# A fused attention block on one core: later weight scans, sooner gate casts, another order at the second step of a batch

## Chip, core and metric

The kernel runs on one core of one Trainium2 chip. The metric is device time in microseconds, from the start to the end of one execution. The engines named below are TensorE (PE, matmuls), VectorE (DVE), ScalarE (ACT), GpSimd (POOL) and SyncE (SP, which issues DMAs).

## What is computed

One encoder layer over 1024 tokens of width 1024. A projection `h = x @ W_in` gives queries, keys, values and gates for two groups of eight heads with 64 columns each. Group a attends within a two-dimensional neighbourhood (rows of 64 tokens, a window of 8 x 16) with a learned bias; group b attends within 128 positions, with rotary positions, a learned sink, and keys and values shared by four heads.

```python
s = einsum(q_r, k_win) * scale + bias              # group a, per grid row
s = where(|i - j| <= 128, einsum(q, k_band) * scale, MASK); s = concat(s, sink)   # group b
y = einsum(softmax(s), v)
mixed = concat([y_a * silu(z_a), y_b * silu(z_b)])
x = layer_norm(alpha * x + mixed @ W_out) * gain + bias
```

Matmul operands are float16 pairs, a high and a low part. Each product is three matmuls: high x high, high x low and low x high. So every operand is scaled, cast (the high half, mostly on ScalarE) and subtracted (the low half, on VectorE or GpSimd), and the scales need the largest absolute value of the weights: that is a scan.

## The kernel before, in words

A first part of about 120 us loads x and the weights, computes the values and projects the first six tiles of 128 columns. Then comes the main loop, which the change is about; a final part finishes the output projection, the residual and the normalisation.

The loop runs over 128 units: 64 of group b, then 64 of group a. A unit is 128 queries of one head with all the keys that they see. Four units make a batch, so there are 32 batches (also called quads, number q covers steps 4q to 4q+3). The loop is written as steps `i`, one per unit, and the engines' orders follow the order in which a step's code emits instructions:

- `batch` and `stage_mm` (L930) emit the score products of four units into PSUM banks with tag `s`, of which there are five. This is done at the end of the step before the batch.
- `stage_qk` (L955, VectorE) adds the bias or mask and takes the row's extreme, into `sn` and `nm`.
- `stage_exp` (L971, ScalarE) takes the exponentials and their sums, for most units back into the PSUM bank; the third unit of a batch goes to an SBUF tile `px`.
- `stage_sum` (L977 and L978, VectorE) makes the reciprocals `ri` of two units' sums.
- `stage_tr` scales and splits the probabilities: high half on ScalarE (L989), low half on VectorE (L990), then a transposing DMA on SyncE (L996) into `tr`.
- `stage_pv` (L1032) multiplies by the values, into one half of the single bank `t`; batch q's comes at step 4q+11 (`PV_AT`), right after the next scores.
- `stage_z` (L1040 and L1043, VectorE) multiplies that half by the gates, at step 4q+13 (`Z_AT`).

Between these, `pump_to` feeds TensorE with other matmuls, spread over the steps by the table `FILL_AT`: first the remaining projections (`FILL`, 48 matmuls of 512 columns each, L401, two PSUM banks with tag `pj`), then the first parts of the output projection (`out_head`, L1162). Evacuations of projected tiles, weight splits (`w_split`, L211 to L217), scans and casts wait in queues, one for each engine; `pop` takes a few of them per step, those with the smaller `prio` first.

Of the output weights, `wo_load` brings in the raw tiles at steps `WO_LD`, `wo_scan` (L430) takes the absolute sums, `wo_max` at step `WO_MAX` combines them, a transpose in the batch that starts at `WO_MAX + 4` and `wo_scale` make the scale, and `wo_split` (`WO_AT`, L1118 to L1131) casts. `m_queue` (`M_AT`, L1146 and L1147) casts the finished gate products of group b, two ScalarE casts and two GpSimd subtractions for each of four tiles. `big_tile` hands out slots of the tags `xb` and `xc`, four each, which held weights before.

Of the kernel before, what the change touches and what calls it, by code (L numbers as in the profile page):

```python
# [38 lines left out]
SCALE_AT = ((4, 6), (7, 2))  # L39
K_ORDER = (5, 0, 6, 1, 7, 2, 3, 4)  # L40
FILL = ORDER[NPRO:]
FILL_AT = [0, 8, 17, 25, 33, 41, 49, 57, 65.5, 74, 82, 90, 98, 106, 113, 121, 124, 126, 128, 131, 136]
ZTAG = {"z3": "zv", "zb3": "zc", "z2": "zs", "zb1": "zd", "zb2": "ze"}
X2POOL = (1, 3, 5)
WVPOOL = (3, 5)
# [1 line left out]
WIN_AT = [186, 202, 218, 234]  # L47
VA_AT = [46, 49, 52, 55]
WO_TAG = ("wor", "wor", "raw", "raw") + ("wr",) * 5 + ("wor", "wor", "raw", "raw", "raw", "wr", "wr")
M_AT = [105, 112, 118, 120]  # L50
WO_PRE = (9, 10, 12, 13, 14, 15)
WO_POST = (7, 8)
WO_MAX = 72
EO = (4, 5, 6, 7, 0, 1, 2, 3)
LAST = ((0, 384), (384, 128))
NPE = 384
PRE_AT = (12, 20)
WARP = (0, 0.33, 0.54, 0.86, 1)
QK_AT = 0.75
WO_AT = [80, 84, 88, 92, 128, 129, 130, 131]  # L60
WO_LD = [18, 22, 26, 30, 36, 39, 42, 45, 48, 112, 116, 33, 130, 130]
WIN0 = (0, 8, 24, 40)
WINW = (24, 32, 32, 24)
# [8 lines left out]
def hybrid_block(ctx, tc, xT, x, wt, wv, wo, bias, sink, gain, lbias, cos, sin, bmask, out):  # L72
# [4 lines left out]
    big = ctx.enter_context(tc.tile_pool(name="big", bufs=4))  # L77
# [15 lines left out]
    def big_tile(name, shape, dt):  # L93
        n = taken[0]
        taken[0] += 1
        return big.tile(list(shape), dt, tag="xb" if n % 8 < 4 else "xc", name=name)

    xh, xl, x1, x1pair, x16h, x16l = {}, {}, {}, [], {}, {}
    for k in range(KT):
# [65 lines left out]
    def enq(eng, fn, *deps, prio=1, after=0):  # L165
        op = Op(eng, fn, deps, prio)
        if clock["step"] is not None:
            queues[eng].append(op)
        elif after:
            events.setdefault(ran[0] + after, []).append(op.emit)  # L170
        else:
            op.emit()
        return op
# [3 lines left out]
    def pop(eng, n, top=1, late=0):  # L177
        q = queues[eng]
        ready = [op for op in q if op.prio <= top and all(
            d.step is not None and d.step + d.lag < clock["step"] + late for d in op.deps)]  # L180
        ready = sorted(ready, key=lambda op: op.prio)[:n]
        for op in ready:
            q.remove(op)
            op.emit()
        return len(ready)
# [243 lines left out]
    def wo_scan(n):  # L429
        nc.scalar.activation(scrap[:, :512], wo_raw[n], AF.Abs, accum_out=wom[:, n:n + 1])  # L430
# [501 lines left out]
    def stage_qk(u):  # L932
        g, p, j, t = u
        n, _c = geom(u)
        ps = st[u, "ps"]
        m, end = n, 384
        if g == "a":
            b, half = t
            m, end = NROW[half] * WINW[b], 384 if half else 384 - WINW[1]
            bias_t, op = st.pop((u, "b"))  # L940
            need(op)
            init = 3e38
        else:
            bias_t = bm[:, 128 if t == 0 else 0:(128 if t == 0 else 0) + n]
            h = 2 * p + j
            init = nsk[:, h:h + 1]
        s0 = sns[units.index(u) % 2]
        sn = s0[:, end - m:]
        if g == "b" and t == 0:
            nc.vector.tensor_copy(s0[:, 384:385], nsk[:, h:h + 1])  # L950
        elif units.index(u) == 64:
            nc.vector.memset(s0[:, 384 - WINW[1]:384], -NEG)
        nm = ap.tile([128, 1], F32, tag="nm", name="nm", bufs=6)
        c = min(p, 1) if g == "b" else 2
        nc.vector.tensor_tensor_reduce(sn[:, :m], ps[:, :m], bias_t, sg[:, c:c + 1], init,  # L955
                                       op0=ALU.add, op1=ALU.min, accum_out=nm)
        st[u, "sn"] = sn
        st[u, "nm"] = nm

    def stage_exp(u):  # L960
        n, _c = geom(u)
        m = n + 1 if u[0] == "b" else n
        sn, nm = st.pop((u, "sn")), st.pop((u, "nm"))
        pt = st[u, "bank"] = st.pop((u, "ps"))
        if units.index(u) % 4 == 2:
            pt = ap.tile([128, 388], F32, tag="px", name="px", bufs=1)
        k = units.index(u) % 2
        if units.index(u) % 2 == 0:
            st["sm"] = ap.tile([128, 2], F32, tag="sm", name="sm", bufs=4)
        sm = st["sm"][:, k:k + 1]  # L970
        nc.scalar.activation(pt[:, :m], sn[:, :m], AF.Exp, bias=nm, scale=-1.0, accum_out=sm)  # L971
        st[u, "p"] = pt

    def stage_sum(us):
        ri, sm = ap.tile([128, 2], F32, tag="ri", name="ri", bufs=4), st["sm"]
        c = st.pop((us[1], "bank"))[:, 508:510]
        nc.vector.tensor_scalar_mul(c, sm, 1.0 / PSCALE)  # L977
        nc.vector.reciprocal(ri, c)  # L978
        for k, u in enumerate(us):
            st[u, "ri"] = ri[:, k:k + 1]  # L980
# [166 lines left out]
            m_ops[e].append(enq("pool", lambda h=h: nc.gpsimd.tensor_sub(  # L1147
                ml[e][:, h], zt[e][:, h], mh[e][:, h]), o))

    LO = 8  # L1150
    NU = len(units)
    def out_mms(t, a, ps, es, c=None):
        o, w = (0, 512) if c is None else LAST[c]
# [162 lines left out]
        stage_mm(us)  # L1316

    PV_AT = {4 * q + 11: q for q in range(30)}
    PV_AT.update({131: 30, 133: 31})
    Z_AT = {4 * q + 13: q for q in range(30) if q not in (24, 25)}  # L1320
    Z_AT.update({115: 24, 116: 25, 132: 30, 134: 31})

    clock["step"] = 0
    scan_ops = []
    for i in range(-LD, NU + LO):
        if 0 <= i + LD < NU:
            stage_load(units[i + LD], i)
        if i < 0:
            continue
        clock["step"] = i  # L1330
        per, h = divmod(i, 16)
        bulk["step"] = i
        if i in VA_AT:
            gather_v(0, VA_AT.index(i))
        for n in range(len(WO_LD)):
            if WO_LD[n] == i:
                load_ops["wo", n] = enq("sp", lambda n=n: wo_load(n), wo_ops.get({9: 0, 10: 1, 12: 2, 13: 3}.get(n)),
                                        w_ops.get(17 + n if 4 <= n <= 8 else None))
                if n not in WO_PRE + WO_POST:
                    scan_ops.append(enq("act", lambda n=n: wo_scan(n), load_ops["wo", n]))  # L1340
        if i in PRE_AT:
            n = len(WO_PRE) - len(PRE_AT) + PRE_AT.index(i)
            scan_ops.append(enq("act", lambda n=n: wo_pre(n)))
        if i == WO_MAX - 6:
            for n in WO_POST:
                scan_ops.append(enq("act", lambda n=n: wo_scan(n), load_ops["wo", n]))
        if i == WO_MAX:
            need(*scan_ops)
            wo_max()
        for n in range(len(WO_AT)):  # L1350
            if WO_AT[n] == i:
                wo_split(n)
        if i == 131:
            enq("sp", gain_load, *m_ops[4])
        if i in M_AT:
            m_queue(4 + M_AT.index(i))
        if bulk["last"] != i or (queues["sp"] and i - queues["sp"][0].born > 2):
            pop("sp", 1 if i < 118 else 3)
        if i < NU:
            if i == 0:  # L1360
                batch(0)
                stage_qk(units[0])
            if i % 4 != 3:
                stage_qk(units[i + 1])
        if i in Z_AT and i % 4 == 3:
            stage_z(Z_AT.pop(i))
        if i > Z3_END:
            pop("dve", 1, 0)
        if i % 4 and i < NU:
            stage_exp(units[i])  # L1370
        early = pop("act", 1, 0) if i % 4 == 1 else 0
        if i % 4 == 1 and i < NU:
            stage_sum(units[i - 1:i + 1])
        if i in Z_AT:
            stage_z(Z_AT.pop(i))
        if i % 4 == 1 and i < NU:
            for u in units[i - 1:i + 1]:
                stage_tr(u)
        if i % 4 == 0 and 4 <= i <= NU:
            for u in units[i - 2:i]:  # L1380
                stage_tr(u)
        early = early or pop("act", 1, 0)
        if i in M_SCALE:
            m_scale(M_SCALE.index(i))
        if WO_MAX + 4 <= i < WO_MAX + 7:
            wo_scale(i - WO_MAX - 4)
        pump_to(i + F1)
        if i - 1 in PV_AT and quad(PV_AT[i - 1])[0] == "a":
            _, p, b = quad(PV_AT[i - 1])
            if p < 3:  # L1390
                gather_v(p + 1, b)
        free = 2 if i % 4 > 1 or i >= NU else 0
        turned = pop("dve", free if i < M_AT[1] else 1 + free)
        if i % 4 == 0 and i < NU:
            stage_exp(units[i])
        if i in PV_AT or i % 4 == 3 and i + 1 < NU:
            if i < NU:
                stage_sum(units[i - 1:i + 1])
            pump_to(i + QK_AT)
            if i + 1 < NU:  # L1400
                batch(i + 1)
            if i in PV_AT:
                stage_pv(PV_AT[i])
            if i + 1 < NU:
                stage_qk(units[i + 1])
        pop("act", max(free + (1 if free and (i >= M_AT[0] or len(queues["act"]) > 4) else 0) - early, 0))
        if not turned:
            pop("dve", 1, 0, 1)
        pop("pool", NP)
        pump_to(i + 1)  # L1410
# [78 lines left out]
```

## Time and profile before

| | us |
|---|---|
| median of 3 runs | 447.92 (447.80 to 448.05) |
| the profiled execution | 448.15 |
| its span, first to last instruction | 446.3 |
| TensorE busy | 434.3 |
| VectorE busy | 347.3 |
| ScalarE busy | 298.5 |
| GpSimd busy | 212.3 |

The profile is one execution. A row of the timeline gives start, duration, engine, line of the kernel, operation, what it writes and reads, the shape and a count of merged instructions; in brackets stands how long the engine had been idle and what ended that. A row of the groups ends in busy time, mean ns of one, and idle time before. A row of the windows gives the stretch, its length, and busy time with the count of instructions for PE, PEld, DVE, ACT and POOL, then the granted clock, the DMA share and GB/s. The granted TensorE clock was 0.999 of full speed.

### The profile page before, as it was taken

The numbers are of one execution on the slowest core, as the hardware profiler recorded it, in microseconds if no ns is written. First come the engines' busy times: TensorE is split into PE (matmuls) and PEld (weight loads), VectorE is DVE, ScalarE is ACT, GpSimd is POOL, SyncE is SP. The second block draws the span as 40 slices with busy tenths as digits, with TensorE's granted clock in tenths as the row PEclk, the third lists the DMA queues.
The fourth block names the chain that finished last, engine by engine and source line by source line (L and its number), as shares of the span: only waits on it lengthen the run. The fifth ranks groups of instructions, "written<-read, shape, count | busy, mean of one in ns | idle before, by whom it ended". The sixth has DMA issues, their size and how long they took to land. (4 is left out here: it accounts for less than half of the span.)

```text
span 446.3 us, 8786 instructions
## 1 busy us (share of the span) xinstructions
PE 434.3 (97%) x2955; PEld 233.7 (52%) x2955; DVE 347.3 (78%) x897; ACT 298.5 (67%) x697; POOL 212.3 (48%) x204
## 2 busy tenths in 40 slices
PE   9999999999998999999999999999999989999994
PEld 9987754444444444444544555454545544444442
DVE  5999948649978888898888888877758849089953
ACT  7798269766588888888867978787867794002211
POOL 1206734546835737557505436654555358005740
PEclk9999999999999999999999999999999999999999
DMA  8991078977946867796978999998898989001711
GB/s 298 325 359 51 25 263 252 320 252 241 317 95 136 140 146 176 128 139 151 172 152 191 166 176 226 200 217 174 213 238 170 193 151 393 6 0 72 258 73 70
DMA packets 133981, 81.72 MB, mean 183 GB/s; under 512 B 101296, under 2 KB 113328, under 8 KB 133680
## 3 DMA queue, kind: packets, MB, share of 16 engines
q1 hardware_dynamic: 133504, 80.67, 72.3%
q8 instruction: 23, 0.38, 0.4%
q10 hardware_dynamic: 432, 0.49, 0.3%
q14 instruction: 22, 0.18, 0.2%
HBM read 50.73 MB, written 9.96 MB: 136 GB/s over the span
## 5 line engine op out<-in xcount | busy, mean ns | idle before, releaser
L401 PE MATMUL ps_pj<-xf,wh 128*128 128x512 f16 x672 | 200.5, 379 | 0.0
L401 PE MATMUL ps_pj<-xf,wl 128*128 128x512 f16 x336 | 127.6, 380 | 0.0
L401 PEld LDWEIGHTS <-wh 128*128 128x128 f16 x672 | 65.2, 98 | 75.0 <-issue 0.5
L989 ACT ACTIVATE split<-ps_s,ri 128x384 f16<-128x384 f32 (+2 forms) x96 | 48.4, 538 | 22.5 <-issue 9.7
L990 DVE SCALAR_TENSOR_TENSOR split<-ps_s,ri,split 128x384 f16<-128x384 f32 (+2 forms) x96 | 52.0, 569 | 12.8 <-ACT split L989 12.8
L1162 PEld LDWEIGHTS <-m 128*128 128x128 f16 x408 | 38.7, 98 | 43.7
L971 ACT ACTIVATE ps_s<-sn,nm 128x385 f32<-128x385 f32 (+3 forms) x96 | 52.1, 543 | 12.7 <-DVE nm L955 11.4
L1162 PE MATMUL ps_s<-wo,m 128*128 128x512 f16 (+1 forms) x240 | 53.3, 374 | 0.0
L401 PEld LDWEIGHTS <-wl 128*128 128x128 f16 x336 | 32.8, 98 | 38.9 <-issue 0.6
L216 POOL TENSOR_SCALAR wr<-wr,wsc 128x512 f32<-128x512 f32 x26 | 22.3, 859 | 50.9 <-ACT wh L211 50.6
L930 PE MATMUL ps_s<-ks,qs 64*128 64x384 f16 (+4 forms) x384 | 36.9, 305 | 3.2 <-DVE split L990 2.9
L955 DVE CUSTOM_DVE_ANT_0 sn<-ps_s,bm,nsk 128x384 f32<-128x384 f32 (+1 forms) x64 | 39.6, 633 | 0.1
L955 DVE CUSTOM_DVE_ANT_0 sn<-ps_s,bias,sg 128x264 f32<-128x264 f32 (+1 forms) x64 | 33.9, 546 | 6.9 <-PE ps_s L930 6.4
L898 POOL TENSOR_SCALAR bias<-bias,rsg 128x552 f32<-128x552 f32 (+1 forms) x24 | 19.8, 826 | 40.1 <-DMA bias<-in_bias 31.4
L217 POOL TENSOR_TENSOR wl<-wr,wh 128x512 f16<-128x512 f32 x26 | 31.9, 1228 | 2.2
L1219 ACT ACTIVATE sd<-mv,eps 128x1 f32<-128x1 f32 x8 | 2.4, 294 | 44.5 <-DVE mv L1217 42.2
L930 PEld LDWEIGHTS <-qs 64*128 64x128 f16 x384 | 16.8, 94 | 25.6 <-issue 19.2
L1261 POOL TENSOR_TENSOR xr<-xr,gb 128x512 f32<-128x512 f32 x7 | 11.2, 1608 | 36.0 <-ACT xr L1258 36.0
L990 DVE SCALAR_TENSOR_TENSOR split<-px,ri,split 128x384 f16<-128x384 f32 (+2 forms) x32 | 27.2, 849 | 1.3 <-ACT split L989 1.3
L678 PEld LDWEIGHTS <-xf 128*128 128x128 f16 x216 | 21.0, 98 | 8.4 <-DVE xf L532 0.3
L977 DVE TENSOR_SCALAR ps_s<-sm 128x2 f32<-128x2 f32 x64 | 10.2, 160 | 18.7 <-ACT ps_s L971 18.3
L1162 PE MATMUL ps_pj<-wo,m 128*128 128x512 f16 (+1 forms) x120 | 24.2, 347 | 0.0
(213 smaller groups left out, 803.1 us busy)
## 6 DMA issues: line engine op xcount, KB each, us to landing
ws<-in_wt SPq DMA_DIRECT2D x15, 512.0 KB, 5.5
wr<-in_wt SPq DMA_DIRECT2D x26, 256.0 KB, 3.2
bias<-in_bias SPq DMA_DIRECT2D x16, 276.0 KB, 3.3
wor<-in_wo SPq DMA_DIRECT2D x16, 256.0 KB, 3.4
xr<-in_x SPq DMA_DIRECT2D x8, 512.0 KB, 7.5
xraw<-in_xT SPq DMA_DIRECT2D x15, 256.0 KB, 4.9
out<-xr SPq DMA_DIRECT2D x14, 256.0 KB, 2.0
bias<-in_bias SPq DMA_DIRECT2D x8, 368.0 KB, 3.6
```

The lines of the kernel that those rows point to most:

```text
L216: nc.gpsimd.tensor_scalar(raw, raw, scale, 1.0, op0=ALU.mult, op1=ALU.mult)
L217: nc.gpsimd.tensor_sub(l, raw, h)
L401: nc.tensor.matmul(ps, a[:, k % 4, :], mv, start=(k == 0 and i == 0), stop=(k == KT - 1 and i == 2))
L678: nc.tensor.matmul(ps[:, :320], lh[t // 4, k][:, 128 * (t % 4):128 * (t % 4) + 128], rh[k][:, 320 * a:320 * a + 320], start=(k == first an ...
L898: op = enq("pool", lambda: nc.gpsimd.tensor_scalar(bv, bv, rsg, -1.0, op0=ALU.mult, op1=ALU.mult), ld, prio=0)
L930: nc.tensor.matmul(st[u, "ps"][:, :m], *parts[i], start=i == 0, stop=i == 2)
L955: nc.vector.tensor_tensor_reduce(sn[:, :m], ps[:, :m], bias_t, sg[:, c:c + 1], init, op0=ALU.add, op1=ALU.min, accum_out=nm)
L971: nc.scalar.activation(pt[:, :m], sn[:, :m], AF.Exp, bias=nm, scale=-1.0, accum_out=sm)
L989: nc.scalar.activation(hl[:, :m, 0, :c], src, AF.Copy, scale=ri)
L990: nc.vector.scalar_tensor_tensor(hl[:, :m, 1, :c], src, ri, hl[:, :m, 0, :c], op0=ALU.mult, op1=ALU.subtract)
L1162: nc.tensor.matmul(ps, lh[:, ts], rh[:, cs], start=(e == EO[0] and i == 0), stop=(e == EO[-1] and i == 2))
L1261: nc.gpsimd.tensor_mul(xr[:, h1], xr[:, h1], gb[:, h1])
```

## The change

- The scans of eight output-weight tiles are queued at steps of their own (`WO_SCAN`, 52 to 78) instead of with their loads (18 to 45). `WO_MAX` goes from 72 to 88, the two last scans with it, and the first four weight splits from steps 80, 84, 88 and 92 to 96, 99, 103 and 107.
- The casts of the four b gates start at steps 64, 72, 80 and 88 instead of 105, 112, 118 and 120. `BIG_TAG` writes out the slots' tags, with other ones for the tiles from number 15 on.
- In a batch's second step (`i % 4 == 1`) the sums of its first two units are emitted before the third unit's `stage_qk`; their split and transposes come before `stage_z`, and the one queued ScalarE operation of that step is popped after both.
- The last value products go from step 133 to 135, gate product 28 from 125 to 127, number 31 from 134 to 136, and the loop has two more steps. The pacing table changes from step 113 on.
- Two conditions on the number of queued operations popped change: the steps are written as 105, and the queue's length is 6 instead of 4.

```diff
-FILL_AT = [0, 8, 17, 25, 33, 41, 49, 57, 65.5, 74, 82, 90, 98, 106, 113, 121, 124, 126, 128, 131, 136]
+FILL_AT = [0, 8, 17, 25, 33, 41, 49, 57, 65.5, 74, 82, 90, 98, 106, 113.5, 122.5, 125, 127, 128.5, 131.5, 136]
-M_AT = [105, 112, 118, 120]
+M_AT = [64, 72, 80, 88]
-WO_MAX = 72
+WO_MAX = 88
-WO_AT = [80, 84, 88, 92, 128, 129, 130, 131]
+WO_AT = [96, 99, 103, 107, 128, 129, 130, 131]
+BIG_TAG = (("xb",) * 4 + ("xc",) * 4) * 2
+BIG_TAG = BIG_TAG[:15] + ("xc", "xb", "xb", "xb", "xc", "xc", "xb", "xc")
+WO_SCAN = {0: 52, 1: 56, 2: 60, 3: 64, 4: 67, 5: 70, 6: 74, 11: 78}
-        return big.tile(list(shape), dt, tag="xb" if n % 8 < 4 else "xc", name=name)
+        return big.tile(list(shape), dt, tag=BIG_TAG[n], name=name)
-    LO = 8
+    LO = 10
-    PV_AT.update({131: 30, 133: 31})
-    Z_AT = {4 * q + 13: q for q in range(30) if q not in (24, 25)}
-    Z_AT.update({115: 24, 116: 25, 132: 30, 134: 31})
+    PV_AT.update({131: 30, 135: 31})
+    Z_AT = {4 * q + 13: q for q in range(30) if q not in (24, 25, 28, 29)}
+    Z_AT.update({115: 24, 116: 25, 127: 28, 129: 29, 132: 30, 136: 31})
-                if n not in WO_PRE + WO_POST:
-                    scan_ops.append(enq("act", lambda n=n: wo_scan(n), load_ops["wo", n]))
+            if WO_SCAN.get(n) == i:
+                scan_ops.append(enq("act", lambda n=n: wo_scan(n), load_ops["wo", n]))
+        if i % 4 and i < NU:
+            stage_exp(units[i])
         if i < NU:
             if i == 0:
                 batch(0)
                 stage_qk(units[0])
+            if i % 4 == 1:
+                stage_sum(units[i - 1:i + 1])
             if i % 4 != 3:
                 stage_qk(units[i + 1])
         if i in Z_AT and i % 4 == 3:
             stage_z(Z_AT.pop(i))
         if i > Z3_END:
             pop("dve", 1, 0)
-        if i % 4 and i < NU:
-            stage_exp(units[i])
-        early = pop("act", 1, 0) if i % 4 == 1 else 0
-        if i % 4 == 1 and i < NU:
-            stage_sum(units[i - 1:i + 1])
-        if i in Z_AT:
-            stage_z(Z_AT.pop(i))
         if i % 4 == 1 and i < NU:
             for u in units[i - 1:i + 1]:
                 stage_tr(u)
         if i % 4 == 0 and 4 <= i <= NU:
             for u in units[i - 2:i]:
                 stage_tr(u)
-        early = early or pop("act", 1, 0)
+        if i in Z_AT:
+            stage_z(Z_AT.pop(i))
+        early = pop("act", 1, 0)
-        turned = pop("dve", free if i < M_AT[1] else 1 + free)
+        turned = pop("dve", free if i < 105 else 1 + free)
-        pop("act", max(free + (1 if free and (i >= M_AT[0] or len(queues["act"]) > 4) else 0) - early, 0))
+        pop("act", max(free + (1 if free and (i >= 105 or len(queues["act"]) > 6) else 0) - early, 0))
```

## The prediction, made before the changed kernel ran

> **What bounds the kernel now.** I read the page first, then the groups, then what TensorE waited for, then the timeline of TensorE batch by batch, and ScalarE and VectorE around one late batch.
>
> ```profile
> span 446.3 us, 8786 instructions
> PE 434.3 (97%) x2955; PEld 233.7 (52%) x2955; DVE 347.3 (78%) x897; ACT 298.5 (67%) x697; POOL 212.3 (48%) x204
> ...
> PE ps_s L930 <- DVE split L990: 2.9, 10, 1.0
> ```
>
> TensorE is busy for 97% of the span, and the change removes no matmul. What can be won is only time in which TensorE stands still. The third row names the largest such wait inside the loop: the score products (L930) wait for VectorE's low half of the split (L990), because that instruction is the last reader of a PSUM bank that the next batch's scores need. The row undercounts: matmul ends are modelled, so I measure a late batch from the start of its scores to the start of its value products (L1032), and take a punctual batch's time away.
>
> ```profile
> 140.35 0.92 PE L930 MATMUL ps_s<-ks,qs 64*128 64x384 f16 x6
> ...
> 143.15 1.01 PE L1032 MATMUL ps_t<-tr,vb 128*64 128x256 f16 x18
> ...
> 148.74 0.96 PE L930 MATMUL ps_s<-ks,qs 64*128 64x256 f16 x7
> ...
> 150.48 1.18 PE L1032 MATMUL ps_t<-tr,vb 128*64 128x256 f16 x24
> ...
> 179.76 0.50 PE L930 MATMUL ps_s<-ks,qs 64*128 64x256 f16 x6
> ...
> 181.51 0.52 PE L1032 MATMUL ps_t<-tr,vb 128*64 128x256 f16 x6
> ...
> 210.12 0.50 PE L930 MATMUL ps_s<-ks,qs 64*128 64x256 f16 x6
> ...
> 211.30 0.65 PE L930 MATMUL ps_s<-ks,qs 64*128 64x384 f16 x5 [0.21 <-DVE split L990]
> 211.88 0.41 PE L1032 MATMUL ps_t<-tr,vb 128*64 128x256 f16 x4
> ...
> 218.28 1.15 PE L930 MATMUL ps_s<-ks,qs 64*128 64x384 f16 x12
> 219.36 0.52 PE L1032 MATMUL ps_t<-tr,vb 128*64 128x256 f16 x5
> ...
> 239.67 0.51 PE L930 MATMUL ps_s<-ks,qs 64*128 64x264 f16 x6
> ...
> 241.52 0.52 PE L1032 MATMUL ps_t<-tr,vb 128*64 128x256 f16 x6
> ...
> 262.09 0.88 PE L930 MATMUL ps_s<-ks,qs 64*128 64x264 f16 x12
> 262.90 0.41 PE L1032 MATMUL ps_t<-tr,va 96*64 96x256 f16 x4
> ```
>
> Punctual batches take 219.36 - 218.28 = 1.08 us (group b's width) and 262.90 - 262.09 = 0.81 us (the narrow windows of group a). The first late batch (number 3) took 2.80 us, 1.7 too long; batches 4, 8 and 12 took 1.74, 1.75 and 1.76, 0.67 too long each, and batch 6 between them is like these; the last of this kind (batch 16, the first of group a) took 1.85, 1.04 too long. Six late batches cost 1.7 + 4 x 0.67 + 1.04 = 5.4 us. Five lie in group b; after batch 16 group a's batches are punctual until the last one.
>
> Why batch 12 was late stands in the timelines of ScalarE and VectorE:
>
> ```profile
> 204.33 0.63 ACT L430 ACTIVATE scrap<-wor 128x512 bf16<-128x512 f32 x1
> ...
> 208.24 0.19 ACT L971 ACTIVATION_READ_ACCUMULATOR ps_s<-sn,nm 128x1 f32 x1
> 208.34 0.58 ACT L287 ACTIVATE qs<-ps_pj 128x512 f16<-128x512 f32 x1
> 209.49 1.05 ACT L989 ACTIVATE split<-ps_s,ri 128x384 f16<-128x384 f32 x2 [0.58 <-ACT qs L287]
> ...
> 208.59 0.53 DVE L955 CUSTOM_DVE_ANT_0 sn<-ps_s,bm,nsk 128x256 f32<-128x256 f32 x1
> ...
> 209.24 0.17 DVE L978 RECIPROCAL ri<-ps_s 128x2 f32<-128x2 f32 x1
> 209.33 0.47 DVE L1040 SCALAR_TENSOR_TENSOR z<-ps_t,zcol,z 128x256 f32<-128x256 f32 x1
> 210.11 1.14 DVE L990 SCALAR_TENSOR_TENSOR split<-ps_s,ri,split 128x384 f16<-128x384 f32 x2 [0.32 <-ACT split L989]
> ```
>
> The second unit's exponentials, sums included, are done at 208.43. Their reciprocal (L978) comes at 209.24, since the third unit's scores (L955, 0.53 us) stand before it in VectorE's order. ScalarE first does a queued cast (L287), then sits idle for 0.58 us until the reciprocal is there. The gate product (L1040) also stands before the two L990. They end at 211.25, and TensorE's second pair starts at 211.30: it was waiting for exactly this. An output-weight scan (L430, 0.63 us) stood in ScalarE's queue shortly before.
>
> The end of the loop has two more waits:
>
> ```profile
> 349.33 1.29 PE L930 MATMUL ps_s<-ks,qs 64*128 64x264 f16 x12
> 350.55 1.18 PE L1032 MATMUL ps_t<-tr,va 96*64 96x256 f16 x24
> 351.66 3.41 PE L1162 MATMUL ps_pj<-wo,m 128*128 128x512 f16 x15
> 355.54 1.18 PE L1032 MATMUL ps_t<-tr,va 128*64 128x256 f16 x24 [0.47 <-DVE z L1043]
> ...
> 361.54 2.33 PE L1162 MATMUL ps_s<-wo,m 128*128 128x512 f16 x10
> 365.27 1.18 PE L1032 MATMUL ps_t<-tr,va 96*64 96x256 f16 x24 [1.39 <-DMA tr<-split]
> ```
>
> The last value products (number 31) wait 1.39 us for their transposes, number 29 waits 0.47 us for the gate product of number 28, and the last batch of scores is 1.22 - 0.81 = 0.4 us late. With the 5.4 us this makes 7.7 us: the most that the change can give.
>
> **The change, part by part.** *Order at the second step of a batch.* Sums and reciprocal move ahead of the third unit's scores, and the gate product and the queued ScalarE operation move behind both splits. Nothing is added. In batch 12's rows: the reciprocal follows the exponentials' end directly, say at 208.8 instead of 209.24, and the first L990 at about 209.7 instead of 210.11, so 0.4 us sooner, and VectorE's 0.32 us of idling is filled with the third unit's scores. What pays is that third unit: its scores come about 0.35 us later, and whatever evacuation sits in the ScalarE queue about 1.1 us later (two L989). Neither is on the path as long as the projection's two banks are refilled only every 24 matmuls.
>
> *Scans.* Eight of the ten scans of L430 on wor leave steps 18 to 45 and go to steps 52 to 78; the loads stay where they are, the raw tiles are held until their casts anyway, and the maximum that depends on the scans moves with them from step 72 to 88, the first casts that need its scale from 80 to 96. Their first user in TensorE is the output head at step 122.5, and the loads of weights 9 and 10, which wait for the casts of 0 and 1 on SyncE's queue, come at steps 112 and 116, so nobody waits.
>
> ```profile
> L430 ACT ACTIVATE scrap<-wor 128x512 bf16<-128x512 f32 x10 | 6.3, 626 | 0.1
> L1146 ACT CAST m<-z 128x512 f16<-128x512 f32 x8 | 4.6, 620 | 0.0
> L1147 POOL TENSOR_TENSOR m<-z,m 128x512 f16<-128x512 f32 x8 | 9.1, 1159 | 1.7 <-ACT m L1146 1.7
> ...
> 239.70:290.00 50.30, 49.69 (x408) 25.74 (x408) 42.39 (x139) 40.32 (x108) 24.92 (x29) 1.00 1.01 192
> ```
>
> The stretch that loses them gets 8 x 0.63 = 5.0 us of ScalarE back. Batches 6, 8 and 12 lost 0.67 us each; order and scans together (0.4 us a batch, and 5.0 us over some seven batches) exceed that, so I take their 2.0 us as gone. Batches 3 and 4 come before any of these scans and get the order alone: 0.4 us in each of three or four batches, of which I take 1.2 us of their 2.4. Batch 16 keeps some scans before it: 0.8 of 1.04.
>
> *Casts of the b gates.* Eight casts on ScalarE and eight subtractions on GpSimd leave steps 105 to 122 for 64 to 91. The window 239.70 to 290 is about that stretch: ScalarE is busy for 40.3 of 50.3 us, so 10 us are free. Into it go 8 x 0.62 for the casts and five of the scans, 5 x 0.63, out of it go four output-weight casts of about the same length: 8.1 - 2.5 = 5.6 us net. It fits, but ScalarE then stands at 46 of 50 us, and queued operations go in front of the fourth exponential, whose sum VectorE waits for. Bounds: nothing, if all of it falls into idle time; 5.6 us, if none does. I take 1.0, near the lower end, because 4 us still stay free and these batches are punctual now. The order may gain 0.4 us a batch there too, but TensorE cannot use it where it doesn't wait. The new tags put the four m tiles into the slots of the raw weights of k1, q1, k2 and q2, which are cast one tile ahead of projections that start at steps 57 to 82: done by then; if one weren't, ScalarE's queue would stand behind it.
>
> GpSimd's share has a price on VectorE. Where GpSimd works beside it, the low half taken from px slows down:
>
> ```profile
> L990 DVE SCALAR_TENSOR_TENSOR split<-ps_s,ri,split 128x384 f16<-128x384 f32 x18 | 10.5, 611 | 1.9 <-ACT split L989 1.9
> ...
> L990 DVE SCALAR_TENSOR_TENSOR split<-px,ri,split 128x384 f16<-128x384 f32 x6 | 7.3, 1213 | 0.0
> ```
>
> These two are from group b (179.8 to 239.7): same shape, 1213 against 611 ns. Each subtraction that meets such a split may cost 0.6 us of VectorE, 8 x 0.6 = 4.8 us at most, nothing at least; GpSimd is busy for half of the window already, so most is paid today, and it is inside my 1.0. The Trainium skill (SBUF — State Buffer, "Who interferes with whom") says that a VectorE instruction with two SBUF inputs contends with a GpSimd one that reads SBUF, and that whoever comes second is blocked for the whole instruction. The rows agree: px is in SBUF, ps_s is not. By that rule the cost could be an estimated 8 x 1.16 = 9.3 us of blocking instead of 4.8.
>
> *The end.* By the fill table 19 instead of 16 matmuls stand between the scores of batches 30 and 31, and the gate casts no longer crowd steps 105 to 122: the 0.4 us of the last scores go. Between batches 29 and 30 it is 21 instead of 24, 0.65 us less cover where nothing waits now; I cost that at nothing. Value products 31 move from step 133 to 135; by the table 21 instead of 10 output matmuls lie before them, 11 x 0.22 (3.41 / 15 from the row at 351.66) = 2.4 us more cover against a wait of 1.39: gone, with 1.0 us to spare. These matmuls are taken from those that follow number 31, under which VectorE casts group a's gates; some 38 still stand ahead of the first that needs them, and nothing waited for the casts, so I cost it at nothing, and at 0.5 us if the casts are late.
>
> Gate product 28 moves from step 125 to 127, straight in front of value products 29, which wait for it already (the row at 355.54). Two more matmuls (17) stand before 29, 0.43 us of the 0.47. In VectorE's order the product then follows the last unit's scores, so it may end up to 2 us later than today; with the order's 0.4 us and a punctual last batch (0.4 us and the sooner start) I expect the wait at 0.5 to 0.8 us, 0.3 more than now.
>
> Sum: 1.2 + 2.0 + 0.8 + 0.4 + 1.4 = 5.8 us won, 1.0 + 0.3 paid: **4.5 us**. The profiled execution took 448.15 us (span 446.3); the median of the runs, 447.92, is 0.23 less, so the forecast is 443.4. Its own range is 441.5 to 445.5.
>
> **Rivals.** *The bank at the end.* Value products 29 stand still for product 28: 2 us later than now at the worst, and 31's gain is eaten. 443.4 + 1.7 = 445.1. For it: 0.47 us are waited already. Against: the fourth scores come sooner once the batch is punctual. The Trainium skill (PSUM — Partial Sum Buffer, "PSUM bank collisions raise a hardware error") has PSUM guarded by bank and quadrant, not by address; here products 28 and 29 use different halves of one bank, and the trace's wait agrees with that rule. By it the move can't be free. Chance 0.10.
>
> *Order and scans don't reach the wait.* If group b is late for GpSimd's slowing of VectorE (1213 ns) rather than for the order, only the 1.4 + 0.4 at the end and 0.2 of batches 6 to 12 come: 447.9 - 2.0 = 445.9, or 446.9 with the 1.0 for the casts. Against: the 0.58 us of idle ScalarE in batch 12. Chance 0.14.
>
> *ScalarE becomes the bound in group a.* The thirteen operations, queued before the fourth exponential, hold up VectorE's sum and then the next scores. If none hides, and collisions with GpSimd add half of their 4.8, it costs 5.6 + 2.4 = 8.0 instead of 1.0: 443.4 + 7.0 = 450.4. From 1.0 + 4.5 = 5.5 us on, about 0.9 us in each of batches 16 to 21, it decides. For it: 46 of 50 us busy. Against: 4 us stay free, and batches there are punctual now. Chance 0.15.
>
> *Gains and new waits cancel*, or the batch waits move a batch further: 447.9. Chance 0.05.
>
> **How the numbers follow.** The forecast has 0.56 and its time is the prediction. 0.2% is 0.9 us, about what a measurement of this kernel can tell from no change. Faster: 0.56 + 0.10 + 0.14 - 0.01 = 0.79; same 0.05; slower 0.16 (the ScalarE rival and an upper tail). The range goes from 440.2 (447.9 less all 7.7 us) to 448.2, which takes in the three milder rivals and leaves the slower one out.
>
> **What would show it.** Right: the wait of L930 for L990 under 1 us in total, batches 6, 8 and 12 at 1.1 us, ScalarE's idle time before L989 smaller, the order L977, L978, L955, L990, L990, then L1040 in VectorE, the transposes' 1.39 us gone. Wrong: late batches among 17 to 22, with ScalarE above 90% there; a wait of over 1.5 us before value products 29; batch 3 as late as before; the first matmul after the loop waiting for m or wo.

## The result, and the profile after

The changed kernel took 441.78 us in the median (441.74 to 442.50, 4 runs), the kernel before 447.99 in the same comparison: a ratio of 0.9865, with a 95% interval from 0.9848 to 0.9882. It is 6.2 us faster; 4.5 were forecast.

The page and TensorE's waits of the changed kernel (its lines stand three further down than before: scores L933, low half L993, value products L1035, gate product L1043 or L1046):

```profile
span 439.9 us, 8794 instructions
PE 431.4 (98%) x2955; PEld 232.7 (53%) x2955; DVE 345.7 (79%) x897; ACT 298.5 (68%) x697; POOL 213.2 (48%) x204
...
PE ps_s L933 <- DVE nm L958: 0.5, 1, 0.5
PE ps_s L933 <- DVE split L993: 0.5, 2, 0.3
PE ps_t L1035 <- DVE z L1046: 0.4, 1, 0.4
```

The span is 6.4 us shorter with the same 2955 matmuls. The wait of the scores for the low half fell from 2.9 to 0.5 us, and the wait for the transposes is gone. The timeline of TensorE shows three of the batches that the prediction measured:

```profile
140.42 0.33 PE L933 MATMUL ps_s<-ks,qs 64*128 64x384 f16 x1
...
142.93 0.63 PE L1035 MATMUL ps_t<-tr,vb 128*64 128x256 f16 x8
...
207.70 0.99 PE L933 MATMUL ps_s<-ks,qs 64*128 64x256 f16 x12
208.62 0.85 PE L1035 MATMUL ps_t<-tr,vb 128*64 128x256 f16 x12
...
236.31 0.88 PE L933 MATMUL ps_s<-ks,qs 64*128 64x264 f16 x12
237.12 0.90 PE L1035 MATMUL ps_t<-tr,vb 128*64 128x256 f16 x14
```

From the start of the scores to the start of the value products, batch 3 takes 2.51 us (2.80 before), batch 12 takes 0.92 (1.76), batch 16 takes 0.81 (1.85). The same difference for every batch, taken in the timeline from the last other matmul before its scores to the first one after its value products, accounts for the whole gain:

| batch or wait | won, us |
|---|---|
| 3 and 4 | 0.30 + 0.15 |
| 6, 8, 12 | 0.69 + 0.83 + 0.84 |
| 7, 11, 15 | 0.25 + 0.24 + 0.10 |
| 16 | 1.04 |
| 31 | 0.41 |
| value products 29 (gate product 28) | 0.08 |
| value products 31 (transposes) | 1.46 |
| sum | 6.39 |

ScalarE and VectorE just before batch 12, after the change:

```profile
204.79 0.20 ACT L974 ACTIVATION_READ_ACCUMULATOR ps_s<-sn,nm 128x1 f32 x1
205.55 1.05 ACT L992 ACTIVATE split<-ps_s,ri 128x384 f16<-128x384 f32 x2 [0.55 <-ACT ps_s L974]
206.49 0.60 ACT L290 ACTIVATE qs<-ps_pj 128x512 f16<-128x512 f32 x1
...
205.29 0.17 DVE L981 RECIPROCAL ri<-ps_s 128x2 f32<-128x2 f32 x1
205.38 0.52 DVE L958 CUSTOM_DVE_ANT_0 sn<-ps_s,bm,nsk 128x256 f32<-128x256 f32 x1
...
206.16 1.14 DVE L993 SCALAR_TENSOR_TENSOR split<-ps_s,ri,split 128x384 f16<-128x384 f32 x2 [0.25 <-ACT split L992]
207.22 0.47 DVE L1043 SCALAR_TENSOR_TENSOR z<-ps_t,zcol,z 128x256 f32<-128x256 f32 x1
```

The reciprocal now precedes the third unit's scores, which run while ScalarE makes the high halves. The two low halves are done at 207.30, and TensorE's scores start at 207.70 and find their banks free. Before, both ended 1.1 us after the scores had begun (211.25 against 210.12).

ScalarE is idle in front of the high halves for as long as before here (0.55 us, 0.58 before), since the queued cast (L290) now stands behind them and no longer in front. What got shorter is the time from the end of the second unit's exponentials to the first high half: 208.43 to 209.49 before, 1.06 us, and 204.99 to 205.55 after, 0.56 us.

### The profile page after: what moved, and what is told of

The parts are those of the page before. It is cut to its first block, busy times and chain, and to the rows that moved or that the text cites. A ratio compares the mean times of both kernels' runs of the same rounds, so it can differ in the third digit from the quotient of the medians.

```text
span 439.9 us, 8794 instructions
## 1 busy us (share of the span) xinstructions
PE 431.4 (98%) x2955; PEld 232.7 (53%) x2955; DVE 345.7 (79%) x897; ACT 298.5 (68%) x697; POOL 213.2 (48%) x204
## 5 line engine op out<-in xcount | busy, mean ns | idle before, releaser
L993 DVE SCALAR_TENSOR_TENSOR split<-ps_s,ri,split 128x384 f16<-128x384 f32 (+2 forms) x96 | 52.0, 570 | 5.6 <-ACT split L992 4.6
L901 POOL TENSOR_SCALAR bias<-bias,rsg 128x552 f32<-128x552 f32 (+1 forms) x24 | 18.7, 779 | 36.1 <-DMA bias<-in_bias 25.7
L933 PE MATMUL ps_s<-ks,qs 64*128 64x384 f16 (+4 forms) x384 | 34.2, 305 | 1.1 <-DVE nm L958 0.5
L993 DVE SCALAR_TENSOR_TENSOR split<-px,ri,split 128x384 f16<-128x384 f32 (+2 forms) x32 | 25.1, 783 | 3.3 <-ACT split L992 3.3
L933 PEld LDWEIGHTS <-qs 64*128 64x128 f16 x384 | 16.3, 94 | 21.1 <-issue 14.4
```

What stands on the lines that cost most here:

```text
L901: op = enq("pool", lambda: nc.gpsimd.tensor_scalar(bv, bv, rsg, -1.0, op0=ALU.mult, op1=ALU.mult), ld, prio=0)
L933: nc.tensor.matmul(st[u, "ps"][:, :m], *parts[i], start=i == 0, stop=i == 2)
L993: nc.vector.scalar_tensor_tensor(hl[:, :m, 1, :c], src, ri, hl[:, :m, 0, :c], op0=ALU.mult, op1=ALU.subtract)
```

## Experiments

Each kernel was run beside the kernel before on the same chip. "Late" below is time beyond the punctual one of the same batch, read as in the table.

**One part at a time.** The first four kernels put one part of the change into the kernel before.

*The order alone.* The reordered block of the diff, without the two conditions on `pop` behind it. At `i % 4 == 1` this is:

```diff
+stage_exp(units[i])
+stage_sum(units[i - 1:i + 1])
 stage_qk(units[i + 1])
-stage_exp(units[i])
-early = pop("act", 1, 0)
-stage_sum(units[i - 1:i + 1])
-stage_z(Z_AT.pop(i))
 stage_tr(...)   # both units
+stage_z(Z_AT.pop(i))
+early = pop("act", 1, 0)
```

> The kernel before with the new order of a batch's steps alone (sum ahead of the third unit's scores, gate product and queued ScalarE operation behind the two splits). Theory O (VectorE's order makes the batches late): batches 6 to 16 become punctual, 3 and 4 gain about 0.3 and 0.15 us as in the changed kernel, the two waits at the end stay: 448.0 - 4.3 = 443.7 us. Theory S (the scans' load on ScalarE makes them late): batches 6, 8 and 12 stay at about 1.7 us from scores to value products, and about 447 us are measured. If both are needed, something between, with some of the late batches left.

Measured: 443.56 us, ratio 0.9901 (0.9884 to 0.9918). Batches 6 to 16 and 31 are punctual, but for 0.2 us in batch 8; batches 3 and 4 gain 0.29 and 0.15. So theory O holds, and the scans aren't needed. One row of TensorE's timeline shows what came new:

```profile
352.51 1.18 PE L1032 MATMUL ps_t<-tr,va 128*64 128x256 f16 x24 [1.89 <-DVE z L1043]
```

Value products 29 wait 1.89 us for gate product 28, which now stands behind both splits of step 125. The wait for the transposes is gone with it, because value products 31 come later by that: their last transpose lands at 360.01, and they start at 360.78.

*The scans alone.*

```diff
+WO_SCAN = {0: 52, 1: 56, 2: 60, 3: 64, 4: 67, 5: 70, 6: 74, 11: 78}
-WO_MAX = 72
+WO_MAX = 88
-WO_AT = [80, 84, 88, 92, ...]
+WO_AT = [96, 99, 103, 107, ...]
```

> The kernel before with the eight scans at steps 52 to 78 alone (and what hangs on them: the maximum at 88, the first casts from 96). Theory S: batches 6, 8 and 12 become punctual, 3 and 4 do not change, 16 gets no better as three scans now stand before it: 448.0 - 2.4 = 445.6 us. Theory O: these batches stay late by over 0.4 us each, 447.5 us or more; batch 16 gets later.

Measured: 448.58 us, ratio 1.0008 (0.9995 to 1.0021): no difference. TensorE's wait for the low halves is as long as before:

```profile
PE ps_s L931 <- DVE split L991: 3.0, 10, 0.9
```

Batches 8 and 12 lose 0.66 us less each, batches 10 and 14 0.66 and 0.70 more. Theory S falls: 5 us less of ScalarE work in front of these batches moves the lateness from one batch to another and leaves its sum, so ScalarE's load was not what made these batches late.

*The casts alone.*

```diff
-M_AT = [105, 112, 118, 120]
+M_AT = [64, 72, 80, 88]
-WO_AT = [80, 84, 88, 92, ...]
+WO_AT = [96, 99, 103, 107, ...]
```

with the changed slots, and the two conditions in `pop` at their old steps.

> The kernel before with the casts of the b gates at steps 64 to 88 alone (with the new slots, and the first output-weight casts at 96 to 107 to make room). Theory C (the casts crowded the end): the scores of batch 31 become punctual, 0.4 us, and batches 17 to 22 stay punctual without the new order: 447.5 us. The rival from the prediction (ScalarE becomes the bound in group a): batches 17 to 22 are late by 0.5 us each or more, 449 us or above.

Measured: 448.23 us, ratio 1.0002 (0.9987 to 1.0017). Batches 17 to 30 stay punctual to 0.1 us. Batch 31 stays 0.41 us late. So the casts cost nothing where they go, and taken alone they bring nothing where they come from, but for 0.65 us less at the transposes and 0.16 at products 29. The time does not show these: in the profiled execution the loop's first scores start 0.9 us later than before (123.11 against 122.19), and the interval is about as wide. Theory C had the price right and the gain wrong.

*The end alone.* The changed `FILL_AT`, `PV_AT`, `Z_AT` and `LO`.

> The kernel before with the end alone: value products 31 at step 135, gate products 28 and 31 later, the pacing table, two more steps. Theory E (the cover of eleven more matmuls): the wait of 1.39 us for the transposes goes, and the scores of batch 31 come punctually from pacing: 448.0 - 1.9 = 446.1 us. The rival of the bank (products 29 wait for product 28): that wait grows from 0.5 to 1.5 us or more and eats the gain, 447 us or above.

Measured: 450.26 us (448.13 to 452.04, 12 runs), ratio 1.0044 (1.0027 to 1.0061), so slower in the median. Its profiled execution, at 448.33 us one of its fastest and no slower than the kernel before, shows the predicted rival of the bank:

```profile
356.76 1.18 PE L1032 MATMUL ps_t<-tr,va 128*64 128x256 f16 x24 [1.82 <-DVE z L1043]
```

The wait for the transposes went (1.46 us), the wait for gate product 28 grew from 0.47 to 1.82 us. In this execution the two nearly cancel. Why its other executions are some 2 us longer than the profiled one isn't shown, and stays open.

**Which part of the order.** Two kernels split the order in two.

*The sum ahead alone*: `stage_exp` and, at `i % 4 == 1`, `stage_sum` in front of `stage_qk(units[i + 1])`; gate product and `pop("act", 1, 0)` stay in front of the splits.

> The kernel before with one part of the order alone: the sum and reciprocal of a batch's first two units stand ahead of the third unit's scores on VectorE; the gate product and the queued ScalarE operation stay in front of the splits. Theory O1 (the reciprocal behind the scores is what made ScalarE idle, 0.58 us in batch 12): batches 6 to 16 become punctual, 444 to 445 us. Rival O2 (the queued operation and the gate product in front of the splits cost as much): the low halves come only some 0.2 us sooner, half of the late batches stay, 446 us or more.

Measured: 443.39 us, ratio 0.9885 (0.9869 to 0.9901): as fast as the whole order, by one pair of short instructions that stands one place sooner. Theory O1 holds. TensorE's waits:

```profile
PE ps_t L1032 <- DVE z L1043: 0.7, 1, 0.7
PE ps_s L930 <- DVE nm L955: 0.5, 1, 0.5
PE ps_s L930 <- DVE split L990: 0.5, 2, 0.3
PE ps_t L1032 <- DMA tr<-split: 0.4, 1, 0.4
```

Batches 6 to 16 are punctual to 0.07 us, and the wait at gate product 28 is 0.7 us instead of 1.89.

*The rest of the order alone*: gate product and queued operation behind the splits, the sum behind the scores as before.

> The other part of the order alone: gate product and queued ScalarE operation behind the splits, the sum still behind the third unit's scores. Theory O1: ScalarE still waits for the reciprocal, the batches stay late, 447.5 us or more. Rival O2: half of the late batches become punctual, 446 us or less.

Measured: 451.03 us (448.80 to 451.53), ratio 1.0053 (1.0034 to 1.0072): theory O1's 447.5 us or more. That it is slower than the kernel before neither theory said. ScalarE and TensorE at batch 12, and TensorE's two longest waits in the loop:

```profile
210.70 1.05 ACT L989 ACTIVATE split<-ps_s,ri 128x384 f16<-128x384 f32 x2 [1.07 <-issue]
...
210.84 0.50 PE L930 MATMUL ps_s<-ks,qs 64*128 64x256 f16 x6
211.99 0.32 PE L930 MATMUL ps_s<-ks,qs 64*128 64x384 f16 x1 [0.64 <-DVE split L990]
...
213.09 1.18 PE L1032 MATMUL ps_t<-tr,vb 128*64 128x256 f16 x24
...
PE ps_s L930 <- DVE split L990: 4.3, 10, 0.9
PE ps_t L1032 <- DVE z L1043: 2.3, 1, 2.3
```

Batch 12 is at 2.25 us instead of 1.76, and the wait for the low halves at 4.3 us instead of 2.9. The first high half comes as long after the exponentials as before (1.06 us). But ScalarE is idle for all of that time, where it did a cast in it before and was idle for 0.58 us: without the sum ahead, the queued operation and the gate product no longer fill the idle time, and are done later. That they are in the way there is argued from the order, not tested by itself.

**What the end needs.** Two kernels join the order to one of the other parts.

> Order and end together, casts and scans as before the change. The order alone left value products 29 waiting 1.9 us for gate product 28, the end alone 1.8 us. Theory C2 (the casts of the b gates at steps 105 to 122 make the last batch's chain on ScalarE and VectorE late, and gate product 28 with it): the wait stays at 1 us or more here, 31's transposes do not wait: about 443.5 us, like the order alone. Rival P (the place of product 28 decides, and step 127 with the new order is soon enough): the wait is at 0.4 us as in the changed kernel, 442 us.

Measured: 443.52 us, ratio 0.9881 (0.9859 to 0.9903), and products 29 wait 1.5 us:

```profile
PE ps_t L1032 <- DVE z L1043: 1.5, 1, 1.5
```

> Order and casts together (first output-weight casts at 96 to 107), scans and end as before the change. Theory C2: the scores' sums of batch 31 start within 1 us of its matmuls instead of 2.9, and value products 29 wait at most 0.5 us; then 31 comes sooner and its transposes make TensorE wait 0.8 to 1.4 us again: about 443 us. Rival P: 29 still waits over 1.2 us, 443.5 us.

Measured: 443.49 us, ratio 0.9888 (0.9870 to 0.9907), with the same wait:

```profile
PE ps_t L1034 <- DVE z L1045: 1.5, 1, 1.5
```

The scans are at their old place in both, which the next experiment shows to be of no weight. Theory C2 gave the first kernel's time and waits, rival P the second's, so neither holds for both. With order and end the last batch's first unit begins 1.78 us after its scores, with order and casts 2.55, in the changed kernel 0.81. The traces show a different obstacle in each. With order and end, the gate casts' subtractions on GpSimd (L1147) meet the low half from px of batch 29, which takes 1.47 us; it takes 0.61 in the changed kernel, where GpSimd has no subtraction there:

```profile
339.38 2.27 POOL L1147 TENSOR_TENSOR m<-z,m 128x512 f16<-128x512 f32 x2
340.59 1.47 DVE L990 SCALAR_TENSOR_TENSOR split<-px,ri,split 128x384 f16<-128x384 f32 x1
```

With order and casts that split takes 0.61 us too, but the last scores come 5.50 us after those of batch 30 instead of 6.36, and an evacuation stands in front of the fourth unit of batch 30 on VectorE, which in the changed kernel comes behind the first unit of batch 31:

```profile
344.74 0.68 DVE L364 SCALAR_TENSOR_TENSOR z<-z,ps_pj 128x512 f32<-128x512 f32 x1
```

So it takes both, the casts out of steps 105 to 122 and the end's new pacing, to make that batch's chain punctual, and only then is gate product 28 soon enough. The casts are worth nothing alone and the end less than nothing; with the order, the two together take the 1.1 us away that each leaves. Both kernels also keep the old conditions on `pop`. These were never run by themselves; from step 112 on old and new do the same.

**Back from the changed kernel.**

*Scans at their loads, all else changed* (`wo_scan` queued in the loop over `WO_LD` again).

> The changed kernel with the eight scans back at their loads (steps 18 to 45); all else as changed. Theory O (the scans' place decides nothing once the sum stands first): batches 6 to 16 stay punctual, 441.8 us within 0.3. Theory S2 (the new order needs the room on ScalarE): some batches between 6 and 12 are late by 0.2 us or more in sum over 0.5 us, 442.5 us or above.

Measured: 441.67 us, ratio 0.9859 (0.9842 to 0.9877), the changed kernel's time. The scans' place decides nothing.

*The sum-only order in the changed kernel* (the gate product and the queued operation in front of the splits again, as in *the sum ahead alone*).

> The changed kernel with the gate product and the queued ScalarE operation back in front of the splits; the sum stays ahead of the third unit's scores. Theory O1 (the sum alone is the gain; the other half is paid for, not earned): as fast as the changed kernel or up to 0.4 us faster where gate product 28 or 29 comes sooner, 441.4 to 441.9 us. Rival: late batches of 0.05 to 0.1 us each appear in 6 to 12 as they did with the sum alone, and the queued casts at 64 to 88 get in front of the splits: 442.3 us or more.

Measured: 442.67 us, ratio 0.9879 (0.9861 to 0.9898), 1.0 us over the kernel with the scans at their loads, which ran beside it. Theory O1 falls: the other half is not only paid for. The rival has the time right, but batches 6 to 16 are punctual, so its late batches did not come; most of the loss is at gate product 28, where the wait is 1.1 us instead of 0.4:

```profile
PE ps_t L1035 <- DVE z L1046: 1.1, 1, 1.1
```

So the late half of the order earns its place only at the end of the loop, together with the casts and the pacing.

**What is left: batches 3 and 4.** They are still late by 1.4 and 0.5 us. The timeline of the changed kernel at the low half of the third unit of batch 2, and of ScalarE beside it:

```profile
137.96 1.52 DVE L993 SCALAR_TENSOR_TENSOR split<-px,ri,split 128x384 f16<-128x384 f32 x1
...
137.93 0.59 ACT L334 ACTIVATE rp_raw<-ps_pj 128x512 f32<-128x512 f32 x1
138.40 0.29 ACT L796 ACTIVATE zg<-zg,gm 128x1 f32<-128x1 f32 x1
138.73 0.29 ACT L797 ACTIVATE zg<-zg,vg 128x1 f32<-128x1 f32 x1
138.93 0.57 ACT L974 ACTIVATE ps_s<-sn,nm 128x385 f32<-128x385 f32 x1
```

*Without qb1's rotation on GpSimd* (in `rope`, the first two calls of the loop return after the shuffle).

> The changed kernel without the two rotary multiplications and the addition on GpSimd for qb1 (both halves; it leaves the rotation of these two heads out). Asks why batches 3 and 4 are still 1.4 and 0.5 us late. Theory G (GpSimd's work blocks VectorE's low half from px, 1.5 us instead of 0.6 in batch 2): that split takes under 0.8 us and batch 3 is late by 0.6 us or less, 441.0 us. Theory L (the chain from scores to split is simply longer than the matmuls between the first batches): batch 3 stays late by 1.2 us or more.

Measured: 442.46 us, ratio 0.9876 (0.9856 to 0.9897), no faster than the changed kernel. The split from px is fast now, VectorE's next sum waits the longer for ScalarE, and batch 3 is as late as it was:

```profile
137.87 0.66 DVE L998 SCALAR_TENSOR_TENSOR split<-px,ri,split 128x384 f16<-128x384 f32 x1
140.17 0.16 DVE L985 TENSOR_SCALAR ps_s<-sm 128x2 f32<-128x2 f32 x1 [1.11 <-ACT ps_s L979]
...
140.32 0.33 PE L938 MATMUL ps_s<-ks,qs 64*128 64x384 f16 x1
...
142.84 0.84 PE L1040 MATMUL ps_t<-tr,vb 128*64 128x256 f16 x12
```

0.66 us instead of 1.52, and 2.52 us from scores to value products instead of 2.51. GpSimd does slow that split, but the split isn't what batch 3 waits for. The next sum stands still for the exponentials on ScalarE, for 1.11 us here and 0.24 in the changed kernel. They start at 138.93 there, behind the three queued operations. Theory L holds. Batch 4 got later by 0.5 us (2.09 instead of 1.59); why isn't shown.

*More projection in front of batch 3, and gate product 28 at step 124.*

```diff
-FILL_AT = [0, 8, 17, 25, 33, 41, 49, 57, 65.5, 74, 82, 90, 98, 106, ...]
+FILL_AT = [0, 7, 15.5, 23.6, 31.6, 39.6, 47.6, 55.6, 64.3, 73, 81.3, 89.6, 97.8, 105.9, ...]
-Z_AT.update({..., 127: 28, 129: 29, ...})
+Z_AT.update({..., 124: 28, 129: 29, ...})
```

> The changed kernel with a pacing table that puts some 7 more projection matmuls in front of batch 3 and 8 in front of batch 4 and gives them back from step 57 on, and with gate product 28 at step 124. Theory L: TensorE fills the waits of batches 3 and 4 (1.4 and 0.5 us) with matmuls that it does later now, group a's batches stay punctual on their spare of 0.7 us and more, products 29 no longer wait (0.4 us): 441.8 - 2.3 = 439.5 us. Rival: the sooner evacuations make the chain later too, or the waits come back in group b or a; then 441 us or more.

Measured: 440.50 us (439.54 to 441.35), ratio 0.9830 (0.9807 to 0.9853). The kernel with the scans at their loads, which is as fast as the changed one, took 441.67 on the same chip, so this is the fastest of all by 1.2 us in the medians (their intervals overlap slightly); the span is 437.7 against 439.9.

```profile
141.66 0.99 PE L933 MATMUL ps_s<-ks,qs 64*128 64x384 f16 x12
142.58 1.01 PE L1035 MATMUL ps_t<-tr,vb 128*64 128x256 f16 x18
...
148.60 0.92 PE L933 MATMUL ps_s<-ks,qs 64*128 64x256 f16 x7
...
150.30 0.74 PE L1035 MATMUL ps_t<-tr,vb 128*64 128x256 f16 x10
```

Batch 3 takes 0.92 us instead of 2.51 and products 29 don't wait any more; batch 4 keeps its lateness (1.70 us, 1.59 in the changed kernel), and small waits come back in batches 16 (0.1 us) and 20 (0.2 us), which gave matmuls up. Theory L holds for batch 3 and not for batch 4; the rival's returning waits came too, but are smaller than the gain. The expected 439.5 us was reached by the profiled execution (439.54) and not in the median.

## Why the prediction was right, and where it was off

**What bounds the kernel, and where the time would come from**: right. All of the gain is TensorE's standing still, and all but 0.59 us of it (batches 7, 11 and 15) is at the places that the prediction listed.

**Order and scans.** The mechanism was right: the reciprocal behind the third unit's scores held up both halves of the split. The sign named for it, less idle time of ScalarE in front of the high halves, shows in the whole span (23.8 us instead of 29.7) but not at batch 12, where the cast left that place. The share given to the scans was wrong. The step said that order and scans together exceed what batches 6, 8 and 12 lose. The order alone does, in it the sum alone (443.4 us), and the scans move nothing (1.0008 alone, 441.67 against 441.78 when put back). The rival that order and scans don't reach the wait, for GpSimd's slowing of VectorE, is out: with the sum alone ahead, the low halves from px in batches 4, 8 and 12 still took about 1.55 us, as before, and the batches behind them were punctual.

**Sizes in the sum.** Batches 6, 8 and 12 brought 2.36 us, not 2.0, and batches 7, 11 and 15 another 0.59 that the prediction didn't count, since it measured batches with two widths against a punctual batch of one width: 1.08 us, where their own is 0.92. Batches 3 and 4 brought 0.45, not 1.2. The forecast took the 0.4 us of batch 12 for every batch. In the timelines the time from the exponentials' end to the first high half fell ahead of batches 3 and 4 only from 0.75 and 0.64 us to 0.49 each, and ahead of batches 5 to 16 from 1.31 to 0.57 in the mean. Batch 16 brought 1.04 instead of 0.8, batch 31 the forecast 0.4, and the transposes 1.46 for 1.4. So the terms err both ways: the rest of the gain was 1.3 us larger, and 1.4 us of price (below) was not paid, against 0.75 us too much for batches 3 and 4. The time is 1.9 us off and not 2.7 because these partly cancel.

**The casts' price**: forecast 1.0 us, measured none. The window of the changed kernel's steps 64 to 91, which answers to the one shown of before:

```profile
236.30:287.00 50.70, 50.70 (x415) 26.21 (x416) 42.61 (x133) 45.96 (x124) 27.44 (x29) 1.00 1.01 190
```

ScalarE is busy for 46.0 of 50.7 us, as worked out (46 of 50), and TensorE for all of it. So even at 91% the free time was enough, and the rival of ScalarE as the bound is out. The collisions with GpSimd were small here: in this stretch the low half from px took 821 ns for 384 columns against 681 in the same stretch before.

```profile
L993 DVE SCALAR_TENSOR_TENSOR split<-px,ri,split 128x384 f16<-128x384 f32 x3 | 2.5, 821 | 0.6 <-ACT split L992 0.6
...
L990 DVE SCALAR_TENSOR_TENSOR split<-px,ri,split 128x384 f16<-128x384 f32 x3 | 2.0, 681 | 0.0
```

The rule that the prediction took from the Trainium skill (SBUF — State Buffer, "Who interferes with whom") agrees with the experiment without the rotation: 1.52 us with GpSimd at work, 0.66 without. That did not decide the time there. It did at the end with order and end alone: the split of 1.47 us instead of 0.61 is most of what makes the last batch's chain 1.0 us later than in the changed kernel.

**The end.** Forecast: 0.3 us more before products 29; measured: 0.08 less. The rows after:

```profile
344.06 0.88 PE L933 MATMUL ps_s<-ks,qs 64*128 64x264 f16 x12
...
345.98 3.84 PE L1165 MATMUL ps_pj<-wo,m 128*128 128x512 f16 x17
350.21 1.18 PE L1035 MATMUL ps_t<-tr,va 128*64 128x256 f16 x24 [0.39 <-DVE z L1046]
...
356.00 4.92 PE L1165 MATMUL ps_s<-wo,m 128*128 128x512 f16 x22
360.85 1.18 PE L1035 MATMUL ps_t<-tr,va 96*64 96x256 f16 x24
...
349.25 0.51 DVE L958 CUSTOM_DVE_ANT_0 sn<-ps_s,bias,sg 128x288 f32<-128x288 f32 x1
349.68 0.48 DVE L1046 SCALAR_TENSOR_TENSOR z<-ps_t,zcol,z 128x256 f32<-128x256 f32 x1
```

The 17 matmuls between products 28 and 29, the last scores straight in front of gate product 28, and the 22 matmuls (one of them ahead by the last rounding) in front of products 31 are as worked out; the wait is shorter because the last batch's chain is punctual. The rival of the bank was real, though: it is what the order alone (1.89 us) and the end alone (1.82 us) run into, and what keeps it away in the changed kernel is the casts and the pacing together, which the prediction named only for the 0.4 us of the last scores.

## What to carry to other kernels

Where two engines hand a chain back and forth, look for the short instruction that the other engine waits for and see what independent work stands in front of it in its own queue: here two operations of 0.3 us together, put ahead of one of 0.5 us, are worth 5 us in 32 batches (443.39 against 448.48). Measure a late stage from start to start, against a punctual stage of the same shape. Try the parts of a change one at a time and together: three of the four parts were worth nothing or less alone, and two of them, only together, add about 1 us to the gain of the first.

## What was not expected of the hardware

TensorE's idle time in the profile falls well short of the time that it lost. In the rows of its scores' waits it went from 2.9 to 1.0 us, and the batches 3 to 31 together became 4.9 us shorter. 9% of spare time on ScalarE was enough for a stretch of 50 us without lateness in any batch. And a collision of VectorE with GpSimd of 0.9 us cost TensorE at most 0.1 us in one place (batches 4, 8 and 12 with the sum alone ahead, 1.55 us instead of 0.61) and held up the last batch by about its length in another (1.47 instead of 0.61).

Which of the two was slowed went by which began first, in these rows by 0.2 us or less. With the sum alone ahead, a subtraction of a weight split on GpSimd (L217) begins 0.02 us before each of these three splits; it takes 1.16 us, and the split about 1.55. With the whole order the split begins 0.09 to 0.20 us before the subtraction and takes 0.61 us; then the subtraction takes 1.43 to 1.54.
